# Expert weights in an MoE layer kernel: down pieces in a ring of their own, split late; a third result tile

## The chip, the cores and the metric

The kernel runs on one core of a Trainium2 chip, in one launch. The metric is the device time of that core in microseconds. A profiled execution is one more execution with the hardware profiler on; its rows are what this document argues from. Engines are named as in the profile: PE (matmul; PEld is its weight load), DVE (VectorE), ACT (ScalarE), POOL (GpSimd), SP (SyncE, which here only issues DMAs). "SPq" is SP's queue of instructions.

## The reference, cut to what matters

One layer: modulated RMSNorm, windowed attention beside a pooling mixer, output projection, residual; then a mixture of experts and a final RMSNorm. The change lies in the mixture of experts. All data are float32.

```python
D_MODEL, SEQ = 1024, 2048
N_EXPERTS, TOP_K, D_EXPERT = 64, 8, 256
def expert_block(args):                       # rows of tokens that chose expert e
    xb = h[tok_b]
    y = (jax.nn.silu(xb @ w_gate[e]) * (xb @ w_up[e])) @ w_down[e]
    return y.astype(F32) * w_b[:, None]
...
routed = zeros(T, D).at[row_tok].add(y_rows)  # gate-weighted, summed over a token's 8 experts
shared = (jax.nn.silu(h @ ws_gate) * (h @ ws_up)) @ ws_down
x = x + g2 * (routed + shared)
return rmsnorm(x, final_g)
```

## The kernel before

After attention and routing (to about 880 us of the span) the kernel runs one list of work, `run(work, ...)`: first the shared expert on 1024 tokens, then the 64 routed experts, large and small ones in turn (the table `CAPS` gives each rank of load a fixed number of rows, 640 down to 128), then the shared expert again on the other 1024 tokens with the final norm. An expert of up to 512 rows is one unit of work, a larger one two.

A unit n goes through these steps. `fetch` gathers its rows by an indirect DMA from POOL (xg<-X). `transpose_x` turns them on PE into xh and xl (PSUM tile tr). `ffn1` multiplies by gate and up weights (PSUM tile g, three of them) and makes fhh and fhl. `ffn2` multiplies by the down weights, in blocks of 128 rows and two halves of 512 columns (PSUM tile y, three of them); for each half DVE writes `yo = y * gate * g2` (line 1170), and after the second half POOL adds the 128x1024 tile into HBM by an indirect DMA (`scatter`, ACC<-yo, line 956). Each scatter waits for the landing of the one before, since all add into ACC. In program order unit n's `ffn2` stands behind `ffn1` of unit n+1.

Every float32 product is three matmuls of a high and a low part (`mm3`, lines 149 to 151). So every weight piece, a tile of 128x1024 (512 KB), is loaded by SP into a raw tile, then split: ACT copies it into the high part (line 145), DVE subtracts (line 146). An expert has six pieces: two of gate, two of up, two of down. Gate and up pieces become gu (six tiles, an expert needs four), down pieces wdh and wdl.

- Raw tiles (`raw_weights`, line 802): a ring of six, raw, and every seventh piece goes to a seventh tile, rawx, whatever it is.
- Results: two tiles yo.
- Down weights: three tiles each of wdh and wdl. `split_down` of expert si+1 stands in program order right behind `split_weights` of si+1.
- Loads: SP issues all six pieces of expert si+2 in the order gate, up, down, and then the row table of a later expert (tb). SP is a queue in order: a load whose raw tile is not free yet holds back all loads behind it.

A scheduler orders the instructions of each engine from this program and assigns the tiles of a ring, so the order on an engine is not that of the code; the order is fixed when the program is built.

Of the kernel before, what the change touches and what calls it, by code (L numbers as in the profile page):

```python
# [10 lines left out]
F32 = mybir.dt.float32  # L11
F32R = mybir.dt.float32r
# [8 lines left out]
P = 128  # L21
D = 1024
# [20 lines left out]
RAWS = 6  # L43
# [49 lines left out]
def layer(ctx: ExitStack, tc, a, rope, cpack, out, stop=99):  # L93
# [693 lines left out]
    with ExitStack() as ph:  # L787
# [11 lines left out]
        last = []  # L799
        pieces, more_raw = [], []  # L800
        g2 = small.tile([P, D], F32, name="g2", bufs=1)
# [3 lines left out]
        def raw_weights(g_src, u_src, d_src):  # L805

            def piece():

                pieces.append(1)
                if len(pieces) % (RAWS + 1) == 0:  # L810
                    if len(pieces) == RAWS + 1:
                        more_raw.append(rawp.enter_context(tc.tile_pool(name="m_rawx", bufs=1, reuse_waits="tile",
                                                                        side="right")))
                    return more_raw[0].tile([P, D], F32, name="rawx", bufs=1)
                return rp_.tile([P, D], F32, name="raw", bufs=RAWS)

            raws = []
            for src in (g_src, u_src):
                for half in range(2):
                    r = piece().rearrange("p (g f) -> p g f", g=2)  # L820
                    SY.dma_start(r, src[:, 2 * half:2 * half + 2])
                    raws.append(r)
            for f in range(2):
                r = piece()
                last[:] = [SY.dma_start(r, d_src[:, f, :])]
                raws.append(r)
            return raws

        def split_weights(raws, ins=None):
            gu = []  # L830
            for r in raws[:4]:
# [7 lines left out]
        def split_down(raws):  # L839
            wd = []  # L840
            for r in raws[4:6]:
                if len(raws) > 6:
                    V.tensor_tensor(r, r, g2, op=OP.mult)
                hi = wp2.tile([P, D], F32R, name="wdh", bufs=3)
                lo = wp2.tile([P, D], F32R, name="wdl", bufs=3)
                split(hi, lo, r)
                wd.append((hi, lo))
            return wd
# [110 lines left out]
        def shared_raw():  # L959
            return raw_weights(by_rows(a["ws_gate"][0:1]),  # L960
                               by_rows(a["ws_up"][0:1]),
                               a["ws_down"][0].rearrange("(c p) f -> p c f", p=P)) + ["scale"]

# [6 lines left out]
        def run(work, between, at):  # L970
# [6 lines left out]
            firsts = []  # L977
            raws = {0: work[0][0]()}
            xs = {0: fetch(*flat[0][3:5]), 1: fetch(*flat[1][3:5])}
            SY.dma_start(g2, bcast(MODS[0:1, 5 * D:6 * D]))  # L980
            gus = {0: split_weights(raws[0], firsts)}
            queue_after(tail["square"], firsts[1][0])
# [7 lines left out]
            for n, (si, ui, nu, rows, load, put) in enumerate(flat):  # L990
# [8 lines left out]
                if n == 0:  # L999
                    with tc.issue_after(lastx[0].ins):  # L1000
                        wds = {0: split_down(raws.pop(0))}
                    between(2)
                    raws[1] = work[1][0]()
# [12 lines left out]
                behind = functools.partial(ffn2, rows, *h, wds[si], put)  # L1016
# [130 lines left out]
        def slot(n, j):  # L1147
# [12 lines left out]
            for o, w in units(CAPS[j]):  # L1160
# [3 lines left out]
                def put(b, r, n, py, y, o=o, n_=n):  # L1164
                    q = (o + b) // P
                    gate = tabs[n_][:r, q, 1:2]
                    if n == 0:
                        y[0] = yp.tile([P, D], F32, name="yo", bufs=2)
                    sl = slice(n * 512, (n + 1) * 512)
                    V.scalar_tensor_tensor(y[0][:r, sl], py[:r], gate, g2[:r, sl], op0=OP.mult, op1=OP.mult)  # L1170
                    if n == 1:
                        scatter(y[0][:r], tabs[n_][:r, q, 0:1].bitcast(I32))
# [106 lines left out]
        def at(n, total, ask=False):  # L1279
# [3 lines left out]
            if u == 1:  # L1283
# [46 lines left out]
```

## Time and profile before

| | us |
|---|---|
| median of 3 runs (2668.33 to 2672.61) | 2668.43 |
| the profiled execution's own time | 2656.01 |
| its span, first to last instruction | 2654.2 |
| PE busy in the span | 2430.7 (92%) |
| DVE busy | 1841.1 (69%) |
| ACT busy | 1215.8 (46%) |
| POOL busy | 854.8 (32%) |
| mean share of the 16 DMA engines, 1015 to 2560 us | 0.83 |

The table's busy times come from the first part of the page, the last row from a view of stretches of time. "Idle before" and "waits" name what ended a wait, inferred from semaphores. In timelines the columns are start, duration, engine, line, operation, out<-in, count, and in brackets the idle time of the engine before the row with its releaser; equal instructions that follow each other are merged in one row, whose duration then runs over all of them. A matmul's recorded time is longer than its spacing, since matmuls are pipelined.

### The profile page before, as it was taken

Reading aid. Unit: us, or ns where it says so; the run is one execution under the profiler, and the core shown is the slowest. Engines: PE = TensorE matmul, PEld = TensorE weight load, DVE = VectorE, ACT = ScalarE, POOL = GpSimd, SP = SyncE. Lnnn points to the kernel's source line nnn. Section 1 sums busy time; section 2 is a strip of 40 time slices with the busy share of each in tenths; the row PEclk is TensorE's granted clock in tenths of the full one; section 3 lists DMA queues with packets and bytes.
Section 4 is the critical chain, followed back from the end, with each engine's and each line's share of the span. In section 5 each row is a group of like instructions: output and inputs, shape, how many; then the busy total and the mean of one; then the engine's idle time right before and its main releaser. Section 6 shows DMA issues by size and latency. Waiting matters only on the chain. (4 is left out here: it accounts for less than half of the span.)

```text
span 2654.2 us, 40459 instructions
## 1 busy us (share of the span) xinstructions
PE 2430.7 (92%) x14397; PEld 2102.8 (79%) x14397; DVE 1841.1 (69%) x3802; ACT 1215.8 (46%) x2052; POOL 854.8 (32%) x681
## 2 busy tenths in 40 slices
PE   6898978999999888999989989999999999999997
PEld 2776766777777677887778889989898888888886
DVE  7898766989899844556655656666665666667667
ACT  5322337777676433344333434444443444444443
POOL 3343332344443332232323332322333333333210
PEclk8999999999999999999989999999999999999998
DMA  7777559444454568778867878898887987888876
GB/s 253 217 243 235 180 159 279 140 140 132 139 152 126 182 190 200 198 225 229 240 181 216 229 200 247 220 273 232 238 247 214 272 242 233 233 248 242 231 204 248
DMA packets 266840, 564.53 MB, mean 213 GB/s; under 512 B 42966, under 2 KB 97950, under 8 KB 266636
## 3 DMA queue, kind: packets, MB, share of 16 engines
q1 hardware_dynamic: 177580, 350.08, 38.4%
q0 software_dynamic: 88768, 210.80, 34.7%
q8 instruction: 114, 1.87, 0.3%
q10 hardware_dynamic: 288, 1.05, 0.1%
q14 instruction: 90, 0.74, 0.1%
HBM read 408.83 MB, written 153.01 MB: 212 GB/s over the span
## 5 line engine op out<-in xcount | busy, mean ns | idle before, releaser
L149 PE MATMUL g<-xh,gu 128*128 128x256 f32 (+12 forms) x2112 | 670.8, 318 | 9.0 <-ACT xh L145 4.7
L150 PE MATMUL g<-xl,gu 128*128 128x256 f32 (+12 forms) x2112 | 658.4, 312 | 6.3 <-DVE xl L146 5.6
L151 PE MATMUL g<-xh,gu 128*128 128x256 f32 (+12 forms) x2112 | 658.0, 312 | 0.0
L956 POOL DMA_INDIRECT ACC<-yo,tb x165 | 307.3, 1862 | 932.1 <-DVE yo L1170 295.7
L149 PEld LDWEIGHTS g<-xh,gu 128*128 128x128 f32 x2112 | 405.9, 192 | 23.2 <-ACT xh L145 5.1
L150 PEld LDWEIGHTS g<-xl,gu 128*128 128x128 f32 x2112 | 406.7, 193 | 18.9 <-DVE xl L146 6.7
L1170 DVE SCALAR_TENSOR_TENSOR yo<-y,tb,g 128x512 f32<-128x512 f32 (+5 forms) x330 | 237.3, 745 | 255.6 <-DMA ACC<-yo,tb 203.5
L151 PEld LDWEIGHTS g<-xh,gu 128*128 128x128 f32 x2112 | 405.7, 192 | 8.7
L146 DVE TENSOR_TENSOR gu<-raw,gu 128x1024 fp32r<-128x1024 f32 x226 | 274.7, 1222 | 144.3 <-ACT gu L145 143.3
L149 PE MATMUL y<-wdh,fhh 128*128 128x512 f32 (+5 forms) x724 | 298.5, 413 | 63.8 <-DVE yo L1170 53.8
L145 ACT ACTIVATE gu<-raw 128x1024 fp32r<-128x1024 f32 x226 | 238.0, 1059 | 171.8 <-PE g L151 106.6
L150 PE MATMUL y<-wdl,fhh 128*128 128x512 f32 (+5 forms) x724 | 292.1, 404 | 0.0
L151 PE MATMUL y<-wdh,fhl 128*128 128x512 f32 (+5 forms) x724 | 291.3, 403 | 0.0
L146 DVE TENSOR_TENSOR xl<-tr,xh 128x512 fp32r<-128x512 f32 (+5 forms) x330 | 207.4, 648 | 80.7 <-ACT xh L145 80.1
L145 ACT ACTIVATE xh<-tr 128x512 fp32r<-128x512 f32 (+5 forms) x330 | 179.9, 566 | 161.4 <-PE tr L877 160.9
L952 POOL DMA_INDIRECT xg<-X,tb x165 | 180.8, 1096 | 160.0 <-PE tr L877 108.0
L145 ACT ACTIVATE wdh<-raw 128x1024 fp32r<-128x1024 f32 x114 | 116.6, 1053 | 231.8 <-PE y L151 230.8
L149 PEld LDWEIGHTS y<-wdh,fhh 128*128 128x128 f32 (+5 forms) x724 | 135.5, 187 | 107.1 <-DVE yo L1170 65.8
L877 PE MATMUL tr<-identr,xg 128*128 128x128 f32 (+6 forms) x1320 | 149.5, 243 | 27.3 <-DVE xl L146 24.4
L877 PEld LDWEIGHTS tr<-identr,xg 128*128 128x128 f32 (+6 forms) x1320 | 138.1, 141 | 43.6 <-DVE xl L146 29.4
L151 PEld LDWEIGHTS y<-wdh,fhl 128*128 128x128 f32 (+5 forms) x724 | 136.0, 188 | 36.2 <-issue 1.0
L150 PEld LDWEIGHTS y<-wdl,fhh 128*128 128x128 f32 (+5 forms) x724 | 136.2, 188 | 30.1 <-issue 0.5
(333 smaller groups left out, 4614.9 us busy)
## 6 DMA issues: line engine op xcount, KB each, us to landing
raw<-in_w_up_dram SPq DMA_DIRECT2D x110, 512.0 KB
raw<-in_w_down_dram SPq DMA_DIRECT2D x110, 512.0 KB
raw<-in_w_gate_dram SPq DMA_DIRECT2D x109, 512.0 KB
wa<-in_w_ada_dram SPq DMA_DIRECT2D x48, 512.0 KB
xt<-in_x_dram SPq DMA_DIRECT2D x32, 512.0 KB
kw<-Kd POOLq DMA_DIRECT2D x14, 768.0 KB, 8.0
rawx<-in_w_gate_dram SPq DMA_DIRECT2D x19, 512.0 KB
rawx<-in_w_up_dram SPq DMA_DIRECT2D x18, 512.0 KB
```

The source lines that it names most:

```text
L145: return (A.activation(hi, src, AF.Copy), E.tensor_tensor(lo, src, hi.bitcast(F32), op=OP.subtract))
L146: E.tensor_tensor(lo, src, hi.bitcast(F32), op=OP.subtract))
L149: T.matmul(ps, lh, rh, start=first, stop=False)
L150: T.matmul(ps, lh, rl, start=False, stop=False)
L151: T.matmul(ps, ll, rh, start=False, stop=last)
L877: T.transpose(tr[:, k, :r], xg[:r, (4 * u + k) * P:(4 * u + k + 1) * P], identr[:r, :r])
L952: G.indirect_dma_start(out=xg, out_offset=None, in_=X2, in_offset=bass.IndirectOffsetOnAxis(ap=idx, axis=0))
L956: G.indirect_dma_start(out=ACC, out_offset=bass.IndirectOffsetOnAxis(ap=idx, axis=0), in_=y, in_offset=None, compute_op=OP.add)
L1170: V.scalar_tensor_tensor(y[0][:r, sl], py[:r], gate, g2[:r, sl], op0=OP.mult, op1=OP.mult)
```

## The change

1. The down pieces leave the ring of raw: they get a ring of two, rawd. The ring raw keeps its six tiles, now for gate and up alone; rawx goes.
2. Down weights are split one expert later in program order: `down_of(si)` stands behind `ffn1` of expert si's own first unit (and behind `ffn2` of the unit before), no longer behind the gate and up split of si one expert earlier. wdh and wdl have two tiles each in place of three.
3. `load_weights(si + 2)` issues only gate and up pieces; the down pieces of si+1 are issued behind them by a closure that `raw_weights` returns.
4. Every third result tile is yox, a tile of its own, so results rotate over three tiles.
5. At the end, two of the tiles for the final norm come from the final pool ("room") in place of wdh and wdl.

The memory is the same: 7 + 6 + 2 = 15 tiles of 4 KB per partition before, 6 + 2 + 4 + 3 = 15 now.

```diff
-            def piece():
-                pieces.append(1)
-                if len(pieces) % (RAWS + 1) == 0:
...
-                    return more_raw[0].tile([P, D], F32, name="rawx", bufs=1)
-                return rp_.tile([P, D], F32, name="raw", bufs=RAWS)
             raws = []
             for src in (g_src, u_src):
                 for half in range(2):
-                    r = piece().rearrange("p (g f) -> p g f", g=2)
-                    SY.dma_start(r, src[:, 2 * half:2 * half + 2])
+                    r = rp_.tile([P, D], F32, name="raw", bufs=RAWS).rearrange("p (g f) -> p g f", g=2)
+                    last[:] = [SY.dma_start(r, src[:, 2 * half:2 * half + 2])]
                     raws.append(r)
-            for f in range(2):
-                r = piece()
-                last[:] = [SY.dma_start(r, d_src[:, f, :])]
-                raws.append(r)
-            return raws
+            def down():
+                ds = []
+                for f in range(2):
+                    r = rp_.tile([P, D], F32, name="rawd", bufs=2)
+                    last[:] = [SY.dma_start(r, d_src[:, f, :])]
+                    ds.append(r)
+                return ds
+            return raws, down
+        def out_tile(n):
+            if n is not None:
+                downs.append(n)
+                if len(downs) % 3 == 0:
...
+                    return more_room[0].tile([P, D], F32, name="yox", bufs=1)
+            return yp.tile([P, D], F32, name="yo", bufs=2)
...
-                hi = wp2.tile([P, D], F32R, name="wdh", bufs=3)
-                lo = wp2.tile([P, D], F32R, name="wdl", bufs=3)
+                hi = wp2.tile([P, D], F32R, name="wdh", bufs=2)
+                lo = wp2.tile([P, D], F32R, name="wdl", bufs=2)
...
-                if ui == 0 and si + 1 < len(work):
-                    gus[si + 1] = split_weights(raws[si + 1])
-                    wds[si + 1] = split_down(raws.pop(si + 1))
-                    if si + 2 < len(work):
-                        raws[si + 2] = work[si + 2][0]()
+                if ui == 0:
+                    if si:
+                        wds[si] = down_of(si)
+                    if si + 1 < len(work):
+                        gus[si + 1] = split_weights(raws.pop(si + 1))
+                        if si + 2 < len(work):
+                            load_weights(si + 2)
+                        if si:
+                            downs_in[si + 1] = downs_in[si + 1]()
...
-                        y[0] = yp.tile([P, D], F32, name="yo", bufs=2)
+                        y[0] = out_tile(n_)
...
-                        room += [wp2.tile([P, D], F32, name=t, bufs=3) for t in ("wdh", "wdl")]
+                        room += [fin["p"].tile([P, D], F32, name="room", bufs=2) for _ in range(2)]
```

What the scheduler makes of it on SP, at an expert of 352 rows in the middle of the list. The numbers tell tiles apart; the rows that load registers are left out. DVE in a wait means an earlier split, a DMAHW name the landing of a load some seven issues back. Before:

```order
L821 DMA raw_19322<-in_w_gate_dram 128x2x512 [waits DMAHW2_49,DMAHW0_49]
L821 DMA raw_19324<-in_w_gate_dram 128x2x512
L821 DMA raw_19326<-in_w_up_dram 128x2x512 [waits DMAHW3_49,DVE_49]
L821 DMA raw_19328<-in_w_up_dram 128x2x512 [waits DMAHW4_49,DVE_49]
L825 DMA raw_19330<-in_w_down_dram 128x1024 [waits DMAHW0_49,DVE_49]
L825 DMA raw_19332<-in_w_down_dram 128x1024 [waits DMAHW5_49,DMAHW1_49,DVE_49]
L1144 DMA tb_19334<-TAB_65 128x4 [waits DMAHW6_49,DMASW1_49,DMASW0_49]
L821 DMA rawx_19592<-in_w_gate_dram 128x2x512 [waits DMAHW7_49,DVE_49]
L821 DMA raw_19594<-in_w_gate_dram 128x2x512
L821 DMA raw_19596<-in_w_up_dram 128x2x512
L821 DMA raw_19598<-in_w_up_dram 128x2x512 [waits DMAHW2_49]
L825 DMA raw_19600<-in_w_down_dram 128x1024 [waits DMAHW3_49]
```

The same place now:

```order
L812 DMA raw_19310<-in_w_gate_dram 128x2x512
L812 DMA raw_19312<-in_w_gate_dram 128x2x512 [waits DMAHW7_49]
L812 DMA raw_19314<-in_w_up_dram 128x2x512 [waits DMAHW0_49]
L812 DMA raw_19316<-in_w_up_dram 128x2x512 [waits DMAHW1_49]
L1165 DMA tb_19318<-TAB_65 128x4 [waits DMAHW2_49,DMASW1_49,DMASW0_49]
L819 DMA rawd_19329<-in_w_down_dram 128x1024 [waits DMAHW4_49,DMAHW3_49,DVE_49]
L819 DMA rawd_19331<-in_w_down_dram 128x1024 [waits DMAHW5_49,DVE_49]
L812 DMA raw_19580<-in_w_gate_dram 128x2x512
L812 DMA raw_19582<-in_w_gate_dram 128x2x512 [waits DMAHW6_49]
L812 DMA raw_19584<-in_w_up_dram 128x2x512 [waits DMAHW7_49]
L812 DMA raw_19586<-in_w_up_dram 128x2x512 [waits DMAHW0_49]
L1165 DMA tb_19588<-TAB_65 128x6 [waits DMASW7_49,DMAHW1_49,DMASW6_49,DMASW5_49]
```

Before, the load into rawx_19592, a gate piece, waits for the split of the down piece rawx_19094 that held the tile, and the loads behind it, which wait for no split, queue behind that. Now the only loads that wait for DVE are the two down pieces, each for the split of the down piece before it in its tile; the four gate and up loads behind them wait for no split of their own. In SP's order the down pieces of one expert stand directly ahead of the gate and up pieces of the expert two further on.

ACT at the same expert (xh is an input part, sg and fhh belong to ffn1). Before:

```order
L145 ACTIVATE fhh_19349<-sg_19392 128x256 [waits DVE_49]
L145 ACTIVATE xh_19346<-tr_19467 128x4x96 [waits PE_49]
L145 ACTIVATE fhh_19350<-sg_19433 128x256 [waits DVE_49]
L145 ACTIVATE wdh_19309<-rawx_19094 128x1024 [waits DMAHW6_49,PE_49]
L145 ACTIVATE wdh_19575<-raw_19330 128x1024 [waits DMAHW4_49,PE_49,Activation_49]
L905 ACTIVATE sg_19653<-g_19621 128x352 [waits PE_49,Activation_49]
L145 ACTIVATE xh_19615<-tr_19646 128x4x128 [waits PE_49]
L145 ACTIVATE gu_19801<-rawx_19592 128x1024 [waits DMAHW7_49]
L145 ACTIVATE gu_19804<-raw_19594 128x1024 [waits DMAHW0_49]
```

Now:

```order
L145 ACTIVATE fhh_19337<-sg_19380 128x256 [waits DVE_49]
L145 ACTIVATE xh_19334<-tr_19455 128x4x96 [waits PE_49]
L145 ACTIVATE gu_19797<-raw_19580 128x1024 [waits DMAHW5_49,PE_49]
L145 ACTIVATE gu_19800<-raw_19582 128x1024 [waits DMAHW6_49,PE_49]
L145 ACTIVATE fhh_19338<-sg_19421 128x256 [waits DVE_49]
L145 ACTIVATE wdh_19551<-rawd_19329 128x1024 [waits DMAHW3_49,PE_49,Activation_49]
L145 ACTIVATE wdh_19555<-rawd_19331 128x1024 [waits DMAHW4_49,PE_49,Activation_49]
L912 ACTIVATE sg_19641<-g_19609 128x352 [waits PE_49,Activation_49]
L145 ACTIVATE xh_19603<-tr_19634 128x4x128 [waits PE_49]
```

The two wdh splits keep their place between two units of ffn1. Before, they were the second down piece of one expert and the first of the next; now they are the two of one expert. The gate split of the coming expert, which at this place stood behind the wdh splits and the first sg, stands ahead of them.

More of the change, by code (lines that the diff above doesn't have):

```diff
@@ L799, in layer @@
         last = []
-        pieces, more_raw = [], []
+        downs, more_room = [], []
         g2 = small.tile([P, D], F32, name="g2", bufs=1)
@@ L805, in raw_weights @@
         def raw_weights(g_src, u_src, d_src):
-            def piece():
-                pieces.append(1)
-                if len(pieces) % (RAWS + 1) == 0:
-                    if len(pieces) == RAWS + 1:
-                        more_raw.append(rawp.enter_context(tc.tile_pool(name="m_rawx", bufs=1, reuse_waits="tile",
-                                                                        side="right")))
-                    return more_raw[0].tile([P, D], F32, name="rawx", bufs=1)
-                return rp_.tile([P, D], F32, name="raw", bufs=RAWS)
             raws = []
@@ L819, in raw_weights @@
                 for half in range(2):
-                    r = piece().rearrange("p (g f) -> p g f", g=2)
-                    SY.dma_start(r, src[:, 2 * half:2 * half + 2])
+                    r = rp_.tile([P, D], F32, name="raw", bufs=RAWS).rearrange("p (g f) -> p g f", g=2)
+                    last[:] = [SY.dma_start(r, src[:, 2 * half:2 * half + 2])]
                     raws.append(r)
-            for f in range(2):
-                r = piece()
-                last[:] = [SY.dma_start(r, d_src[:, f, :])]
-                raws.append(r)
-            return raws
+            def down():
[10 more added lines that the diff above has]
+                if len(downs) % 3 == 0:
+                    if not more_room:
+                        more_room.append(rawp.enter_context(tc.tile_pool(name="m_yox", bufs=1, reuse_waits="tile",
+                                                                         side="right")))
+                    return more_room[0].tile([P, D], F32, name="yox", bufs=1)
+            return yp.tile([P, D], F32, name="yo", bufs=2)
         def split_weights(raws, ins=None):
             gu = []
-            for r in raws[:4]:
+            for r in raws:
                 w = wp.tile([P, 2, 4, DE], F32R, name="gu", bufs=6)
@@ L837, in split_weights, with split_down @@
             return [gu[:2], gu[2:]]
-        def split_down(raws):
+        def split_down(raws, scaled):
             wd = []
-            for r in raws[4:6]:
-                if len(raws) > 6:
+            for r in raws:
+                if scaled:
                     V.tensor_tensor(r, r, g2, op=OP.mult)
-                hi = wp2.tile([P, D], F32R, name="wdh", bufs=3)
-                lo = wp2.tile([P, D], F32R, name="wdl", bufs=3)
+                hi = wp2.tile([P, D], F32R, name="wdh", bufs=2)
+                lo = wp2.tile([P, D], F32R, name="wdl", bufs=2)
                 split(hi, lo, r)
@@ L961, in shared_raw @@
                                by_rows(a["ws_up"][0:1]),
-                               a["ws_down"][0].rearrange("(c p) f -> p c f", p=P)) + ["scale"]
+                               a["ws_down"][0].rearrange("(c p) f -> p c f", p=P))
         def shared_unit(o):
@@ L977, in run, with load_weights, down_of @@
             firsts = []
-            raws = {0: work[0][0]()}
+            raws, downs_in = {}, {}
+            def load_weights(s):
+                raws[s], downs_in[s] = work[s][0]()
+            def down_of(s):
+                return split_down(downs_in.pop(s), s in (0, len(work) - 1))
+            load_weights(0)
+            downs_in[0] = downs_in[0]()
             xs = {0: fetch(*flat[0][3:5]), 1: fetch(*flat[1][3:5])}
             SY.dma_start(g2, bcast(MODS[0:1, 5 * D:6 * D]))
-            gus = {0: split_weights(raws[0], firsts)}
+            gus = {0: split_weights(raws.pop(0), firsts)}
             queue_after(tail["square"], firsts[1][0])
@@ L1000, in run @@
                     with tc.issue_after(lastx[0].ins):
-                        wds = {0: split_down(raws.pop(0))}
+                        wds = {0: down_of(0)}
                     between(2)
-                    raws[1] = work[1][0]()
+                    load_weights(1)
+                    downs_in[1] = downs_in[1]()
                     xt[1], steps = transpose_x(xs.pop(1))
```

## The prediction

> **What bounds the kernel now.** First the page: how busy each engine is.
>
> ```profile
> span 2654.2 us, 40459 instructions
> PE 2430.7 (92%) x14397; PEld 2102.8 (79%) x14397; DVE 1841.1 (69%) x3802; ACT 1215.8 (46%) x2052; POOL 854.8 (32%) x681
> ```
>
> PE sets the pace, and only its idle time and its clock can be won. The change touches the routed experts alone, so next the view of stretches for these, in two stages (columns: stretch, length, busy time of PE, PEld, DVE, ACT, POOL, granted clock, DMA share, GB/s).
>
> ```profile
> 1015.00:1550.00 535.00, 498.39 (x2912) 439.33 (x2911) 314.12 (x415) 209.70 (x309) 163.91 (x110) 0.96 0.78 212
> 1550.00:2560.00 1010.00, 966.39 (x6357) 888.88 (x6356) 663.52 (x884) 446.31 (x662) 312.03 (x209) 0.98 0.85 242
> ```
>
> PE is idle for 535 - 498.39 = 36.6 us and 1010 - 966.39 = 43.6 us, 80 in all. The clock is short by 0.04 x 535 + 0.02 x 1010 = 41.6 us of full clock. These 122 us, less their overlap, are all that can be won. PE's waits in the first stage, then in the second, say who is late:
>
> ```profile
> PE y L149 <- DVE yo L1170: 17.4, 8, 3.9
> PE tr L877 <- DVE xl L146: 16.2, 6, 4.9
> ...
> PE y L149 <- DVE yo L1170: 35.5, 14, 5.5
> PE tr L877 <- DVE xl L146: 7.4, 5, 4.1
> ```
>
> PE waits for DVE, though DVE is busy only 978 of these 1545 us. So DVE, which works in order, is itself held. The waits of DVE, then of ACT, over both stages:
>
> ```profile
> DVE yo L1170 <- DMA ACC<-yo,tb: 197.9, 43, 8.1
> DVE gu L146 <- ACT gu L145: 188.4, 149, 6.9
> ...
> ACT gu L145 <- DMA rawx<-in_w_gate_dram: 48.1, 14, 9.3
> ACT gu L145 <- DMA raw<-in_w_gate_dram: 45.5, 27, 7.0
> ACT gu L145 <- DMA raw<-in_w_up_dram: 11.8, 6, 4.1
> ```
>
> There are two causes. One: DVE cannot write a result because the scatter of the result two blocks earlier hasn't landed. Two: ACT waits for a weight piece, DVE for ACT, and both stand in order before work that PE needs. An instance of the first (timelines of DVE and POOL):
>
> ```profile
> 1048.87 0.75 DVE L1170 SCALAR_TENSOR_TENSOR yo<-y,tb,g 128x512 f32<-128x512 f32 x1 [5.66 <-DMA ACC<-yo,tb]
> ...
> 1038.66 2.40 POOL L956 DMA_INDIRECT ACC<-yo,tb  x1 [6.66 <-DVE sg L922]
> 1049.48 1.58 POOL L956 DMA_INDIRECT ACC<-yo,tb  x1 [6.84 <-DMA ACC<-yo,tb]
> 1056.68 1.57 POOL L956 DMA_INDIRECT ACC<-yo,tb  x1 [4.32 <-DMA ACC<-yo,tb]
> ```
>
> The scatters run one at a time. And of the second (SP, ACT, DVE, PE):
>
> ```profile
> 1858.49 0.33 SPq L1144 DMA_DIRECT2D tb<-TAB  x1
> 1887.10 0.38 SPq L821 DMA_DIRECT2D rawx<-in_w_gate_dram  x1
> 1890.66 0.95 SPq L825 DMA_DIRECT2D raw<-in_w_down_dram  x2
> 1897.64 0.38 SPq L821 DMA_DIRECT2D raw<-in_w_gate_dram  x1
> ...
> 1893.92 1.06 ACT L145 ACTIVATE gu<-rawx 128x1024 fp32r<-128x1024 f32 x1 [6.39 <-DMA rawx<-in_w_gate_dram]
> 1905.07 1.06 ACT L145 ACTIVATE gu<-raw 128x1024 fp32r<-128x1024 f32 x1 [3.56 <-DMA raw<-in_w_gate_dram]
> ...
> 1885.86 1.21 DVE L146 TENSOR_TENSOR wdl<-rawx,wdh 128x1024 fp32r<-128x1024 f32 x1
> 1906.15 1.22 DVE L146 TENSOR_TENSOR gu<-raw,gu 128x1024 fp32r<-128x1024 f32 x1 [3.66 <-ACT gu L145]
> ...
> 1909.13 0.80 PE L149 MATMUL y<-wdh,fhh 128*128 128x512 f32 x1 [5.54 <-DVE yo L1170]
> 1910.15 0.63 PE L151 MATMUL y<-wdh,fhl 128*128 128x512 f32 x1
> ```
>
> SP issues nothing from 1858.8 to 1887.1: rawx still holds a down piece, whose split begins at 1885.86, and the loads behind wait in line. Then two experts' pieces come within 11 us, gate split follows gate load by 7 us, and PE stands for 5.54 us. After it the matmuls take 0.63 us. Because six pieces rotate over seven tiles, rawx falls to the first gate piece once in seven experts; SP's order confirms that place.
>
> **The change part by part.** *The third result tile.* A result now waits for the scatter three blocks back. The row at 1048.87 waited for the scatter issued at 1038.66; now it would need the one before, landed by then, since 1038.66 could not start earlier. In a burst of three or four blocks (an expert's ffn2) a tile gains one whole scatter, 7 to 10 us by the starts above (1038.66, 1049.48, 1056.68), and the longest wait of DVE is 8.1 us. So nearly all of this cause should go. Walking PE's gaps above 0.6 us in the timeline, I put about 31 us of the 80 on it, most in the first stage. Taken: -28.
>
> *Rings apart.* The 29 us hold on SP goes: no gate load waits for a down split of its own tile any more. The gaps behind late weights are about 44 us. Those at the rotation (PE stands 4 to 6 us, seven or eight times) should vanish. Taken: -40, before the cost below.
>
> *The clock.* It fell with the stalls (0.63 us matmuls right behind one). Of 41.6 us about half lies inside the idle time already counted. Taken: -16 of 20.
>
> *Down loads ahead of the gate loads.* This is the cost. The down loads now wait for both splits of the expert before, and behind them on SP stand four weight loads and a table; for the gate pieces ACT waits, for the tables POOL's gathers. An ordinary expert shows the time there is:
>
> ```profile
> 1955.40 2.01 ACT L145 ACTIVATE wdh<-raw 128x1024 fp32r<-128x1024 f32 x2 [3.23 <-PE y L151]
> 1956.76 2.35 DVE L146 TENSOR_TENSOR wdl<-raw,wdh 128x1024 fp32r<-128x1024 f32 x2
> 1958.00 1.52 SPq L821 DMA_DIRECT2D raw<-in_w_gate_dram  x2
> 1968.33 1.06 ACT L145 ACTIVATE gu<-raw 128x1024 fp32r<-128x1024 f32 x1 [0.65 <-PE g L151]
> 1969.77 1.06 ACT L145 ACTIVATE gu<-raw 128x1024 fp32r<-128x1024 f32 x1 [0.38 <-PE g L151]
> ...
> 1887.00:1889.00 2.00, 2.00 (x15) 2.00 (x14) 1.81 (x3) 0.53 (x2) 0.35 (x1) 1.00 0.58 63
> 1889.00:1892.00 3.00, 3.00 (x22) 2.98 (x21) 0.00 (x0) 0.00 (x0) 0.00 (x0) 1.00 1.00 233
> 1892.00:1899.00 7.00, 7.00 (x48) 6.96 (x47) 3.84 (x4) 4.77 (x7) 2.90 (x2) 1.00 1.06 398
> ```
>
> From the first wdl split done (1956.76 + 1.2 = 1958.0) to the two gate splits there are 10.3 and 11.8 us. What the burst of six loads at 1887.10 needed: nothing for 2 us, 3 us shared with an indirect DMA (233 GB/s in all), then 398 GB/s, which is 1.3 us for a piece of 0.52 MB. With half of the 233 for the weights, 0.35 MB are in by 1892, the third piece (1.57 MB) 3.1 us later, so 8 us after the first issue, the fourth at 9.3. ACT saw the first two 1 us later than this sum gives (1893.92 against 1892.5). So the gate pieces, now third and fourth, are usable about 9 and 10.3 us after the first down load: 1 us to spare on average. How late a split may be before PE feels it: at 1905.07 ACT waited 3.56 us and PE stood 5.54; the waits of about 1.5 us on other experts left PE 0 to 1.2 us idle. Bounds: zero if the pieces always make it; 2 us at each of some 45 experts with short units, 90 us, if they never do. I take 0.25 us x 45 = 11, near the lower end, because the mean arrival lies before the deadline, and a longer unit (half of the experts until 2300 us) leaves 4 us more.
>
> [...] The rate of 233 GB/s in the stretch with POOL's transfers agrees with sharing; the next stretch shows that the sharing ends after some 3 us.
>
> *Late split of the down pieces.* Same splits, same count, at the same place on ACT; two tiles are enough since both splits waited for the last ffn2 already ("ACT wdh" waits there, row at 1955.40), and a whole ffn1 covers them. Only at the last routed expert, where two ffn2 follow each other, PE waits for two splits: from 1955.40 to 1956.76 + 2.35 = 3.7 us, of which some part was there before. Taken: +2. The two "room" tiles cost nothing: their loads stand at the same place on SP.
>
> Sum: -28 - 40 - 16 + 11 + 2 = **-71 us** on the profiled execution, whose own time is 2656.0: 2585. The median of the runs is 12.4 above it, so **2597 us**.
>
> **The rivals.** *Late gates on most short experts* (gain partly given back): 1 us at 45 experts in place of 0.25, so 34 us less: 2631. For it: 1 us to spare is little. Against it: longer waits for weights than 1.5 us are seen only at the rotation.
>
> *Slower.* The two down pieces push the gate load past the tolerance on every short expert. It decides when the fourth piece takes over 13 us after the first down load, in place of 10.3: the gates' DVE subtract then stands in front of the evictions of y, PE stands about 2.5 us, and the clock falls with it, 1 us more. 3.5 x 45 = 158 less 84 won: +74, or 2742; with half of these experts hit, 79 - 84 + 2 + some clock, no change. For it: the sixth load of the burst did arrive late behind a scatter. Against it: the up loads that stood third and fourth at 1889 were split without a wait.
>
> *The scatter chain takes over.* Scatters run singly, and a third tile makes none faster.
>
> ```profile
> ACC<-yo,tb POOLq DMA_INDIRECT x165, 7.2
> ```
>
> At 7.2 us to landing and 0.7 to the next start, 162 need 1280 of 1545 us. If the denser weight bursts stretch one to 9.2 us, they need 1604, and nothing is won: about 2668. Against it: DVE waits for scatters for 198 us, not for most of the time, and the same bytes move.
>
> *The order does not change on chip*: excluded by SP's order.
>
> **How the numbers follow.** Forecast case 0.70 (2575 to 2620 alone), late gates 0.15, scatter chain 0.06, slower 0.09. The range of 8 in 10 goes from 2562 (all 80 us idle and 25 of clock won, nothing lost) to 2648. A measurement of this kernel tells 0.2%, 5 us, from no change. Faster 0.86: the first two cases and a little of the chain; same 0.05; slower 0.09.
>
> **What would show it.** In the profile after: DVE's waits for ACC from 198 us to below 50; no stretch of SP over 20 us without a load; ACT's waits for gate and up pieces together from 105 us to below 60, spread thinly over the experts; PE's waits in this stage below 25 us, clock 0.98 to 0.99. Wrong if ACT waits for gate pieces at nearly every expert, if ACC still holds DVE, or if PE's idle time falls without the span.

## The result and the profile after

The changed kernel takes 2584.38 us (median of 4 runs, 2572.22 to 2586.92) against 2668.38 for the kernel before (median of 4 runs as well; the table of the time before has three of them): a ratio of 0.969, 95% interval 0.9662 to 0.9718, or 84 us less. The forecast was 2597, with a range of 2562 to 2648. The profiled execution took 2586.92 us. Its page, and then the view of stretches (columns as before):

```profile
span 2585.0 us, 40372 instructions
PE 2411.0 (93%) x14397; PEld 2090.0 (81%) x14397; DVE 1850.9 (72%) x3802; ACT 1215.3 (47%) x2052; POOL 841.3 (33%) x681
```

```profile
1015.00:1500.00 485.00, 469.31 (x2755) 417.06 (x2756) 297.34 (x390) 200.73 (x297) 147.96 (x102) 0.97 0.79 221
1500.00:2480.00 980.00, 976.00 (x6542) 901.50 (x6541) 685.03 (x904) 455.85 (x678) 314.50 (x218) 1.00 0.90 254
2480.00:2585.00 105.00, 77.23 (x417) 65.62 (x415) 63.26 (x172) 31.82 (x56) 6.20 (x4) 0.90 0.65 205
```

PE is idle for 15.7 us in the first of these stages and for 4.0 in the second, where it was 36.6 and 43.6. The clock is short by 0.03 x 485 = 14.6 us in the first and by nothing in the second. The third row is the end, and there PE is idle for 28 us. The waits of PE in the three stages, then those of DVE and ACT that the prediction named (the routed experts), and SP's:

```profile
PE tr L884 <- DVE xl L146: 10.5, 4, 4.2
PE y L149 <- DVE yo L1191: 4.7, 1, 4.7
...
PE y L149 <- DVE yo L1191: 2.7, 3, 1.1
...
PE g L149 <- issue: 9.5, 1, 9.5
...
DVE yo L1191 <- DMA ACC<-yo,tb: 6.0, 3, 2.2
DVE yox L1191 <- DMA ACC<-yox,tb: 4.5, 1, 4.5
...
ACT gu L145 <- DMA raw<-in_w_gate_dram: 36.8, 23, 4.9
...
SPq L819 <- DVE wdl L146: 1071.1, 128, 39.3
```

DVE's waits for a scatter fell from 197.9 us to 10.5, ACT's for gate pieces from 93.6 to 36.8. SP now stands at the down loads (line 819) for 1071 us in all; the longest of these waits is 39.3 us, ahead of the first routed result, and 25.3 us among the routed experts. That SP stands is not new: before, the waits at its weight loads (lines 821 and 825) came to about 1150 us in the same stretch, up to 34.5 us. What is left is a group of four stalls between 1200 and 1370 us and one stall of 9.5 us behind the experts.

The two executions also differ ahead of the change. The first and the last write of a routed result, before and after (DVE):

```profile
1028.45 2.21 DVE L1170 SCALAR_TENSOR_TENSOR yo<-y,tb,g 128x512 f32<-128x512 f32 x3
...
2570.68 0.75 DVE L1170 SCALAR_TENSOR_TENSOR yo<-y,tb,g 128x512 f32<-128x512 f32 x1
```

```profile
1037.31 2.17 DVE L1191 SCALAR_TENSOR_TENSOR yo<-y,tb,g 128x512 f32<-128x512 f32 x3
...
2493.24 1.41 DVE L1191 SCALAR_TENSOR_TENSOR yox<-y,tb,g 128x512 f32<-128x512 f32 x2 [4.52 <-DMA ACC<-yox,tb]
```

The second row of after holds two writes; the last starts at 2493.91. So the part up to the first result took 8.9 us more (in the kernels below it ends anywhere from 1030 to 1039 on two of the chips, with the change or without, so I do not put this down to the change), the routed part 1456.6 us in place of 1542.2, 85.6 less, and the end, from there to the last instruction, 91.1 in place of 83.5, 7.6 more. In the routed part PE's idle time fell from 81.1 us to 19.2, and the time at half clock from 78.5 us to 27.3, which is 25.6 us of full clock. These lengths, taken in the same way from every profile, are used below: "routed" is the time from the first to the last write of a routed result, "end" the time behind it.

### The profile page after: what moved, and what is told of

Same layout as the page of the kernel before. It is cut to its first block, busy times and chain, and to the rows that moved or that the text cites. A ratio compares the mean times of both kernels' runs of the same rounds, so it can differ in the third digit from the quotient of the medians.

```text
span 2585.0 us, 40372 instructions
## 1 busy us (share of the span) xinstructions
PE 2411.0 (93%) x14397; PEld 2090.0 (81%) x14397; DVE 1850.9 (72%) x3802; ACT 1215.3 (47%) x2052; POOL 841.3 (33%) x681
## 5 line engine op out<-in xcount | busy, mean ns | idle before, releaser
L146 DVE TENSOR_TENSOR gu<-raw,gu 128x1024 fp32r<-128x1024 f32 x264 | 322.7, 1225 | 233.1 <-ACT gu L145 231.0
L149 PEld LDWEIGHTS g<-xh,gu 128*128 128x128 f32 x2112 | 400.8, 190 | 29.6 <-issue 10.1
L150 PEld LDWEIGHTS g<-xl,gu 128*128 128x128 f32 x2112 | 401.5, 190 | 15.9 <-DVE xl L146 4.2
L151 PEld LDWEIGHTS g<-xh,gu 128*128 128x128 f32 x2112 | 401.1, 190 | 8.6
L963 POOL DMA_INDIRECT ACC<-yo,tb x110 | 192.3, 1748 | 626.5 <-DVE yo L1191 155.8
L145 ACT ACTIVATE gu<-raw 128x1024 fp32r<-128x1024 f32 x264 | 279.1, 1059 | 213.9 <-PE g L151 156.4
L149 PE MATMUL y<-wdh,fhh 128*128 128x512 f32 (+5 forms) x724 | 292.2, 404 | 24.3 <-ACT yo L1049 11.3
L145 ACT ACTIVATE wdh<-rawd 128x1024 fp32r<-128x1024 f32 x132 | 132.9, 1053 | 270.3 <-issue 132.1
L1191 DVE SCALAR_TENSOR_TENSOR yo<-y,tb,g 128x512 f32<-128x512 f32 (+5 forms) x220 | 159.5, 745 | 50.5 <-PE y L151 43.4
L963 POOL DMA_INDIRECT ACC<-yox,tb x55 | 95.7, 1740 | 288.1 <-DVE yox L1191 49.6
L146 DVE TENSOR_TENSOR wdl<-rawd,wdh 128x1024 fp32r<-128x1024 f32 x132 | 155.3, 1215 | 21.7 <-ACT wdh L145 21.7
L884 PEld LDWEIGHTS tr<-identr,xg 128*128 128x128 f32 (+6 forms) x1320 | 138.4, 142 | 27.0 <-DVE xl L146 13.4
```

Source lines behind the costliest of these rows:

```text
L145: return (A.activation(hi, src, AF.Copy), E.tensor_tensor(lo, src, hi.bitcast(F32), op=OP.subtract))
L146: E.tensor_tensor(lo, src, hi.bitcast(F32), op=OP.subtract))
L149: T.matmul(ps, lh, rh, start=first, stop=False)
L150: T.matmul(ps, lh, rl, start=False, stop=False)
L151: T.matmul(ps, ll, rh, start=False, stop=last)
L884: T.transpose(tr[:, k, :r], xg[:r, (4 * u + k) * P:(4 * u + k + 1) * P], identr[:r, :r])
```

## The experiments

All times are in us. The kernels were measured in three groups, a, b and c, each on another chip; "before" is the kernel before on the chip of the group. On that of group b it took 2726, and the first routed result of the four kernels comes at 1089 to 1103 in place of 1028 to 1039, while the routed parts are no longer than elsewhere. So kernels of different groups are compared by ratio and by routed length. Lengths and idle times come from one profiled execution of each kernel. Two of the changed kernel differ by 1.6 us in the routed part, 4.2 in its idle time and 2.3 in the end; those of gate_first, on two chips, by 15.4 us in the routed part.

| kernel | group | median | before | ratio (95%) | routed | PE idle in it | end |
|---|---|---|---|---|---|---|---|
| before | | 2668.4 | | | 1542.2 | 81.1 | 83.5 |
| changed | | 2584.4 | 2668.4 | 0.969 (0.9662 to 0.9718) | 1456.6 | 19.2 | 91.1 |
| rings_only | a | 2636.6 | 2666.7 | 0.9874 (0.9832 to 0.9915) | 1508.1 | 56.7 | 87.2 |
| tile_wdl2 | a | 2641.4 | 2666.7 | 0.9896 (0.9854 to 0.9938) | 1512.4 | 60.4 | 94.7 |
| no_rot | a | 2663.6 | 2666.7 | 0.9985 (0.9959 to 1.0011) | 1543.9 | 81.3 | 82.7 |
| no_rot_tile | a | 2573.8 | 2666.7 | 0.9654 (0.9622 to 0.9687) | 1442.4 | 18.3 | 91.1 |
| no_rot_half | b | 2621.2 | 2726.2 | 0.9617 (0.9563 to 0.9671) | 1445.9 | 15.5 | 82.0 |
| gate_first | b | 2614.2 | 2726.2 | 0.961 (0.9554 to 0.9666) | 1425.1 | 0.9 | 91.9 |
| early512 | b | 2648.0 | 2726.2 | 0.9729 (0.9672 to 0.9787) | 1453.9 | 18.6 | 95.4 |
| no_rot_tile_early | b | 2640.1 | 2726.2 | 0.9696 (0.9643 to 0.9749) | 1433.2 | 11.8 | 102.0 |
| after_again | c | 2582.9 | 2669.2 | 0.9682 (0.9651 to 0.9712) | 1455.0 | 23.4 | 88.8 |
| gate_first_again | c | 2556.6 | 2669.2 | 0.9579 (0.9555 to 0.9603) | 1440.5 | 9.7 | 92.6 |
| no_rot_tile_again | c | 2583.2 | 2669.2 | 0.9689 (0.9654 to 0.9724) | 1440.8 | 15.9 | 93.1 |
| after_half | c | 2560.0 | 2669.2 | 0.9598 (0.9558 to 0.9637) | 1438.2 | 11.2 | 87.5 |

### One part of the change at a time

**rings_only**, the changed kernel with two result tiles:

```diff
-                if len(downs) % 3 == 0:
+                if len(downs) % 3 == 3:
```

> The changed kernel with two result tiles again; rings and late split stay. My theory (two separate causes, the third tile worth 28 us of idle time and about 8 of clock): 36 us slower than the changed kernel, about 2620, with DVE's waits for ACC back near 150 to 200 us. Rival, the rings do it all (DVE waited for the scatter only because late splits stood ahead of the results): 2585 to 2595, and DVE's waits for ACC below 60 us. Rival, the tile does it all: about 2660.

**tile_wdl2**, the kernel before with the third result tile. The memory for it comes from one wdl tile, so this is not the tile quite alone:

```diff
+        def out_tile(n): ...                  # as in the change
-                lo = wp2.tile([P, D], F32R, name="wdl", bufs=3)
+                lo = wp2.tile([P, D], F32R, name="wdl", bufs=2)
...
-                        y[0] = yp.tile([P, D], F32, name="yo", bufs=2)
+                        y[0] = out_tile(n_)
```

> The kernel before with the third result tile and nothing else but one wdl tile less, which pays for its memory; the rotation of six pieces over seven tiles stays. My theory: 28 us of idle time and 8 of clock won, about 2632; the gaps of 4 to 6 us at the rotation stay, the waits of DVE for ACC fall below 60 us. Rival, the tile does it all: 2590. Rival, the rings do it all: 2665.

The waits over 1015 to 2560 us, of rings_only and then of tile_wdl2 (of each those of PE, then DVE's for a scatter):

```profile
PE y L149 <- DVE yo L1191: 37.2, 17, 4.3
PE tr L884 <- DVE xl L146: 16.5, 5, 4.1
...
DVE yo L1191 <- DMA ACC<-yo,tb: 151.2, 39, 6.2
```

```profile
PE y L149 <- DVE yo L1181: 29.9, 14, 4.5
PE tr L888 <- DVE xl L146: 19.9, 9, 3.7
PE y L149 <- DVE yox L1181: 9.2, 6, 3.4
...
DVE yo L1181 <- DMA ACC<-yo,tb: 20.9, 5, 8.3
```

Alone, the rings win 34 us of the routed part and the tile 30. Both win less than was expected: 2637 us came in place of 2620 for the rings alone, 2641 in place of 2632 for the tile. The rivals, by which one of the two does it all, fell. But 34 and 30 make 64, and together the two win 86. The 22 us between are a result that the sum in the prediction has no place for. With the rings alone the stalls at the rotation are gone (between 1550 and 2290 us PE's longest gap is 2.4 us, 5.5 before), and in their place PE waits 17 times, 2.2 us each, for a result tile; with the tile alone DVE hardly waits for scatters any more (21.6 us in all), and the late weights stay. A part of the 22 us may be the wdl tile that tile_wdl2 lacks, which was not tried alone: ACT's waits for weight pieces are 154 us there, 105 before.

### Is it the rotation?

**no_rot**, the kernel before without the seventh raw tile; **no_rot_tile** has also the third result tile of tile_wdl2, with three wdl tiles:

```diff
-                if len(pieces) % (RAWS + 1) == 0:
+                if False:
```

> The kernel before without its seventh raw tile: six pieces over six tiles, so that each tile always takes the same piece; the early split and two result tiles stay. My theory (the rotation is the cause of the late weights, not the early split): as the changed kernel with two result tiles, about 2620, and no stretch of 20 us without a load on SP. Rival, the split's place is what counts, and one raw tile less makes weights later: 2668 or more.

> The kernel before without the seventh raw tile, whose memory goes to the third result tile: 6 raw, 6 wdh and wdl, 3 results, as many tiles as before. My theory: nearly all of the gain, 2585 to 2600, since both causes are gone. Rival, rings of their own and the late split are needed: 2630 or more, with PE's waits for xl and y behind late gate pieces as before.

no_rot, over 1015 to 2560 us, and behind it ACT's waits for gate pieces in no_rot_tile:

```profile
PE y L149 <- DVE yo L1170: 61.6, 29, 4.0
...
DVE yo L1170 <- DMA ACC<-yo,tb: 187.8, 41, 8.0
...
ACT gu L145 <- DMA raw<-in_w_gate_dram: 96.2, 47, 4.2
```

```profile
ACT gu L145 <- DMA raw<-in_w_gate_dram: 37.6, 26, 6.0
```

Taking the rotation away does what it should to SP: its longest wait among the routed experts falls from 34.5 us to 16.6. And yet nothing is won (0.9985, an interval that holds 1). PE's idle time is the same 81 us; 61.6 us of it are now 29 waits for DVE's write of a result, where before there were 22 waits of 52.9 us (the two rows in the prediction). With the third tile as well, the routed part is 100 us shorter than before. By the expectation, no_rot should have taken about 2620, the time then expected of rings_only. It took 2664, and the theory that had each cause stand by itself fell here. The rival, which came nearer with its 2668, blamed the early split and the missing raw tile; it fell with no_rot_tile, which has both and takes 2574.

**no_rot_half** asks whether the scatters had taken over. It is no_rot with scatters of half their rows, so that half of each routed result isn't added:

```diff
-                        scatter(y[0][:r], tabs[n_][:r, q, 0:1].bitcast(I32))
+                        scatter(y[0][:r // 2], tabs[n_][:r // 2, q, 0:1].bitcast(I32))
```

> The kernel before without its seventh raw tile, with two result tiles, and each routed scatter adds only the first half of its rows (the other rows of the result are left out). It asks why taking the rotation away won nothing. Theory, the scatter chain had taken over: a scatter takes fewer us, DVE's waits for ACC fall from 188 us to below 60, and the gain appears, 2575 to 2600. Rival, the early split and the tight raw ring still bring weights late: 2650 or more, with PE's waits as they were. Between: 2600 to 2650, both.

```profile
PE y L149 <- DVE yo L1170: 11.6, 13, 3.8
...
DVE yo L1170 <- DMA ACC<-yo,tb: 107.7, 39, 4.3
```

PE's waits for results fall from 61.6 us to 11.6, and the gain appears: the routed part is 98 us shorter than that of no_rot, with two result tiles, six raw tiles and the early split. DVE's own waits for scatters stay at 107.7 us, not below 60 as expected: shorter ones (4.3 us at most, 8.0 in no_rot) seldom reach PE. So in no_rot the scatters were what held the kernel. With half scatters the DMA engines were less busy, too (a share of 0.79 between 1500 and 2480 us, 0.86 in no_rot), so this run doesn't say that it was only the tile's wait; no_rot_tile, where scatters are whole and a tile more stands between, says it from the other side, with 18 us of idle time left.

So the two causes hide one another: these runs show that the gains do not add up. How it happens at each expert was not traced. My reading, argued and not shown, is that behind a late weight piece the scatters have caught up, and no tile is waited for; where weights come in time, the scatters are behind, and a third tile is needed to let DVE go on. In all, DVE waits for scatters about as long in both kernels (197.9 us before, 187.8 in no_rot). The rows show a link the other way round too. With the third tile, ACT's waits for gate pieces fall from 96.2 us to 37.6, though the raw tiles and the order of the loads are the same. That fits a DVE that stands for a scatter, splits late and so frees raw tiles late: a part of the late weights was the scatters' doing.

### What the order of the loads costs

The four stalls that are left look like this one in the changed kernel (SP, ACT, DVE, PE):

```profile
1166.73 1.47 SPq L819 DMA_DIRECT2D rawd<-in_w_down_dram  x2
1168.99 0.97 SPq L812 DMA_DIRECT2D raw<-in_w_gate_dram  x2
1170.14 1.00 SPq L812 DMA_DIRECT2D raw<-in_w_up_dram  x2
1172.45 0.35 SPq L1165 DMA_DIRECT2D tb<-TAB  x1
1192.60 1.47 SPq L819 DMA_DIRECT2D rawd<-in_w_down_dram  x2
1195.17 1.30 SPq L812 DMA_DIRECT2D raw<-in_w_gate_dram  x2
...
1203.94 1.06 ACT L145 ACTIVATE gu<-raw 128x1024 fp32r<-128x1024 f32 x1 [4.00 <-DMA raw<-in_w_gate_dram]
...
1205.02 1.22 DVE L146 TENSOR_TENSOR gu<-raw,gu 128x1024 fp32r<-128x1024 f32 x1 [4.37 <-ACT gu L145]
...
1206.91 0.54 PE L884 MATMUL tr<-identr,xg 128*128 128x128 f32 x4 [3.80 <-DVE xl L146]
```

ACT was free for the gate split 7.3 us after the first down load was issued (4.00 us before 1203.94) and got the piece at 11.3. The prediction had 10.3 us until the piece is needed and 9 until it is there. At the fourth stall PE waits for DVE's write of a result (the row of 4.7 us further up), behind a gate piece for which ACT waited 4.91 us.

**gate_first** puts the gate pieces of an expert ahead of the down pieces:

```diff
                         if si + 2 < len(work):
-                            load_weights(si + 2)
+                            ups_in.pop(si + 2)()
+                        if si + 3 < len(work):
+                            load_gates(si + 3)
                         if si:
                             downs_in[si + 1] = downs_in[si + 1]()
```

> The changed kernel with the gate pieces of an expert issued ahead of the down pieces that stood in front of them (order on SP: gate, down, up, table). Theory, the four stalls of about 4 us between 1200 and 1365 us come from the down loads ahead in the queue: the gates land two pieces, 2.6 us, earlier, which takes about 10 us with the clock, 2575. Rival, gates are late because they share with scatters and gathers: 2584 unchanged. Rival, up pieces, now behind, come late in their place: 2590 or more.

> The changed kernel once more, on the chip and in the call of the next three, so that they can be compared with it. Both theories of the next runs expect its ratio to the kernel before as it was, 0.966 to 0.972, with late gate pieces stopping PE about four times between 1200 and 1370 us and some 9 us at the barrier behind the experts.

after_again came out so: 0.9682, with four stalls of 3.3 to 4.9 us at the same places, and 5.9 us at the barrier in place of 9.

> The kernel with gate pieces ahead of down pieces, beside the changed kernel. Its profile in the first run had none of the four stalls. Theory, the order on the queue is what the change lost: 15 us of idle time and 10 of clock less than the changed kernel, ratio 0.959 to 0.962. Rival, the stalls were absent by chance of that chip: the same as the changed kernel within 5 us, and the stalls are there again.

SP and ACT of gate_first_again at the same expert, its waits (ACT to 2500 us, DVE to 2560), and the stretch in which the stalls were, of this kernel and then of the changed one:

```profile
1176.64 4.07 SPq L812 DMA_DIRECT2D raw<-in_w_gate_dram  x2
1193.76 1.48 SPq L825 DMA_DIRECT2D rawd<-in_w_down_dram  x2
...
1195.39 1.06 ACT L145 ACTIVATE gu<-raw 128x1024 fp32r<-128x1024 f32 x1 [0.43 <-PE g L151]
```

```profile
ACT gu L145 <- DMA raw<-in_w_gate_dram: 2.8, 2, 1.4
...
DVE yo L1208 <- DMA ACC<-yo,tb: 113.5, 35, 7.6
DVE yox L1208 <- DMA ACC<-yox,tb: 45.6, 15, 5.8
```

```profile
1200.00:1500.00 300.00, 300.00 (x1771) 266.66 (x1770) 199.35 (x263) 130.42 (x193) 104.36 (x69) 1.00 0.85 243
```

```profile
1200.00:1500.00 300.00, 284.80 (x1588) 249.04 (x1587) 180.34 (x235) 119.48 (x175) 91.72 (x63) 0.95 0.79 224
```

This kernel beats the changed one: on the same chip 2556.6 against 2582.9, 26 us less, as gate_first_again expected (25); in group b its ratio is 0.961, but the changed kernel has no run there. The expectation of gate_first had only 10 us, because it counted the two pieces ahead in the queue, 2.6 us. The rows show another size: the tile of the first gate piece is free at 1176.64, while in the changed kernel the loads stand until 1195.17 behind two down loads, which wait for the splits of the down pieces before. SP held the first for 18.5 us, not for 2.6. (The trace of the changed kernel says the same by itself: the split that frees this tile ends there at 1175.45.) PE has no idle time at all from 1200 to 1500, and the full clock. The profiled execution of this kernel was the slowest of its five (2573.36); in it two stalls of 2.4 and 2.3 us stand at 2155 and 2247, behind a DVE that waits for a scatter again.

DVE waits for scatters for 159 us there, with three tiles, though PE is idle for only 9.7 us of the routed part. In the profiled execution of gate_first, the fastest of its four, these waits are 35.4 us, and PE is idle for 0.9 us in the whole routed part. It is busy for 1425.1 - 0.9 = 1424.2 us of it, and the changed kernel's 1456.6 - 19.2 = 1437.4, less half of its 27.3 us at half clock, make 1423.7; so by this estimate gate_first lost about nothing to the clock there, and little but PE's own work is left to shorten.

**no_rot_tile_again** stands beside these:

> Six raw tiles without rotation and the third result tile, early split, beside the changed kernel. Theory, it is faster than the changed kernel by about 9 us: 5 at the barrier (its down splits of the last expert stand earlier), 4 in fewer late gates. Rival: the two are equal within 3 us and the difference seen was one of chips.

On one chip it equals the changed kernel (0.9689 and 0.9682), though on different chips it had seemed 10 us faster: the rival held. So a ring of its own for the down pieces, with the late split, is worth no more than the plain ring of six, when three result tiles are there.

### The end

Behind the last expert a loop for overflowing experts stands, with no turn here, at which all engines meet. POOL and PE of the changed kernel there, and then of the kernel before:

```profile
2485.05 1.55 POOL L963 DMA_INDIRECT ACC<-yox,tb  x1 [6.88 <-DVE wdl L146]
2493.87 1.55 POOL L963 DMA_INDIRECT ACC<-yo,tb  x1 [7.27 <-issue]
2500.71 1.55 POOL L963 DMA_INDIRECT ACC<-yo,tb  x1 [5.29 <-DVE fhl L146]
2507.60 1.55 POOL L963 DMA_INDIRECT ACC<-yox,tb  x1 [5.34 <-DMA ACC<-yo,tb]
...
2515.48 0.79 PE L149 MATMUL g<-xh,gu 128*128 128x512 f32 x1 [9.48 <-issue]
```

```profile
2576.28 1.56 POOL L956 DMA_INDIRECT ACC<-yo,tb  x1 [5.23 <-DMA ACC<-yo,tb]
...
2584.04 0.50 PE L149 MATMUL g<-xh,gu 128*128 128x512 f32 x1 [2.50 <-issue]
```

The write of the last result ended at 2494.65, its scatter could start 13 us later, and PE went on at 2515.48. The brackets of three of the changed kernel's four scatters name other releasers. But where the trace has the landing of a scatter, at 2484.32 and at 2506.87, the next starts 0.73 us behind it, at 2485.05 and at 2507.60: a scatter waits for the one before. From 2285.40 to 2507.60 us there are 27 of them, 8.5 us from start to start.

The same two places in every profile say where the end got longer. From the last write's start to the row at which PE goes on it takes 13.4 us before and 21.6 in the changed kernel; from there to the last instruction 70.1 and 69.5. With two result tiles and whole scatters the first stretch is 13.4 to 15.6 us (before, no_rot, rings_only), and one scatter starts in it; with three it is 19.7 to 22.1 in seven profiles, with the early split or the late one, and two scatters start in it (the two kernels with an early unit of 512 rows, below, left aside). So what the end lost is one more scatter in line, which the third tile allows.

**after_half**, the changed kernel with scatters of half their rows (the edit of no_rot_half; half of each routed result isn't added):

> The changed kernel in which each routed scatter adds only the first half of its rows (the other rows of the result are left out). Theory, the scatters standing in line at the end set the barrier: the 9.5 us at the barrier go, with 5 of clock, and nothing between 1500 and 2480 us changes, since PE is busy there: 12 to 20 us below the changed kernel if the late gates stay, 25 to 40 if they go too because the loads no longer share with scatters. Rival, the barrier waits for something else: less than 5 us won and the stall at the barrier stays.

```profile
PE g L149 <- ACT gu L1282: 2.2, 1, 2.2
PE tr L884 <- DVE xl L146: 4.3, 3, 1.7
```

The 9.5 us (5.9 in after_again) became 2.2, with another releaser: the barrier waits for the scatters. From the last write to PE's going on it takes 17.1 us. The kernel is 23 us faster than after_again, between the two ranges that were expected, but little of this is the end's: by the profiles 16.8 us are won in the routed part, 6.1 ahead of it and 1.3 in the end. In the routed part the late gates shrank (waits of 1.7 us at most for xl, 4.2 in the changed kernel) but didn't go. Gate pieces landed there 7.2 us after their issue (median of 128), in the changed kernel 8.7.

**early512** gives PE 256 rows more to do ahead of that barrier, and **no_rot_tile_early** does the same in the other kernel. The line shown is not all of the edit: the stored results take the two gu tiles into which the final norm loaded ahead, so that it has four such tiles in place of six.

```diff
-        fins = [(256, 1024, early_put), (512, 1280, final_put(1280)), (256, 1792, final_put(1792))]
+        fins = [(512, 1024, early_put), (256, 1536, final_put(1536)), (256, 1792, final_put(1792))]
```

> The changed kernel with the last shared expert's early unit, whose results are stored until the scatters are done, of 512 rows in place of 256, and two units of 256 behind it. Theory, PE's 9.5 us at 2506 us are the scatters that still stand in line when the experts are through: 17 us more matmuls ahead of the barrier hide them, 9.5 us and 5 us of clock less, about 2570. Rival, the final norm of 16 tiles behind the barrier sets the end, whatever PE does: 2580 to 2590.

> The kernel before without the seventh raw tile, with the third result tile and with the early unit of 512 rows. Theory: its 5 us at the barrier and 2 us of clock go, about 2566. Rival, the final norm sets the end: 2574 or more.

The stall at the barrier went, to 2.2 us in both. The end became longer: 95.4 against 91.1 and 88.8 of the changed kernel, 102.0 against 91.1 and 93.1 of no_rot_tile. Neither is faster by ratio (0.9729, 0.9696) than the kernel that it came from. Behind the row at which PE goes on, 66.4 and 67.3 us are left, though PE is busy there for only 35.2 and 36.7 us, in place of 52.3 in both kernels that they came from. So PE's work is not what sets this stretch, as the rival had it. That the loads, norms and stores of the 16 last tiles set it is the rival's reading, and was not followed further; nor was what the two tiles less cost.

## Why the prediction was right, and where it was not

**Sum.** -71 was forecast on the profiled execution, and -69 is what the two profiled executions differ by. That match is luck: 9 us were lost ahead of the routed part, and the medians differ by 84. Errors of the terms cancel, too. In the routed part PE's idle time fell by 62 us, where its terms (-28, -40, +11) make 57; the clock gave 25.6 us in place of 16; the end cost 7.6 in place of 2. The direction, the order of size and the two causes were right; the gain was under-sized by 13 us.

**Two causes, 31 and 44 us.** Both were there: each edit wins alone (30 and 34 us of the routed part, of which 20.7 and 24.4 are idle time). What failed is that the sum treated them as separate. I put each gap of PE down to the one cause that ended it. That gives the right total for taking both away (idle time 81 to 19), and too much credit to either alone: no_rot, which takes only the rotation away in its plainest form, wins nothing, because the scatters end the waits in its place.

**The third tile, -28.** The waits that it was to take went: DVE's for scatters are 21.6 us in tile_wdl2 and 10.5 now. But its worth is no fixed number: 20.7 us of idle time alone, 37.5 beside the rings (rings_only to the changed kernel), 63.0 in no_rot. The reason given, that a tile gains one scatter, fits the runs, and fits the end, where one scatter more stands in line.

**Rings apart, -40.** The stalls at the rotation vanished; but rings of their own were not needed for that, since no_rot_tile does as well. That no stretch of SP over 20 us without a load would be left was wrong: there are three, up to 25.3 us. The clock of 0.98 to 0.99 that I named came out as 0.97 in the first stage and 1.00 in the second.

**Down loads ahead of the gate loads, +11.** The step that failed most. The cost was right in kind and wrong in place and size. I took 0.25 us at 45 experts, from the time between splits at one expert at 1955 us. (A small slip in the same sum: ACT saw the first piece 1.4 us later than reckoned, by its own numbers, not 1.) In that part the gate pieces do come in time: ACT waits 16 times, 17.1 us in all, between 1500 and 2480, and PE is idle for 4.0. The price is paid at four places of the first stage, where an expert of 128 rows (256 at the fourth) follows one of 448 to 512, and ACT, in the instance shown, is ready after 7.3 us, not 10.3, and gets the piece at 11.3, not 9. It is 3.8 + 4.2 + 2.1 + 4.7 = 14.8 us of idle time and 27.3 us of half clock behind them, 28 us in all; gate_first_again wins 26 back. And SP holds the gate loads until the down tiles are free, for 18.5 us in the instance shown.

**The upper bound, 90 us.** No run shows the 2 us at each of 45 experts behind it; 28 us were paid. That the weights get half of the rate beside an indirect DMA was my estimate. In the trace of the kernel before they had less: from 1889 to 1892 us the queue of SP's loads (q1) moved 0.29 MB of 0.70 and that of the indirect DMAs (q0) 0.41, and from 1892 to 1897 q1 moved 1.98 MB of 2.00, at 400 GB/s in all. With half scatters (after_half) gate pieces land sooner, after 7.2 us in place of 8.7, so the scatters do bear on them. But in the instance shown the larger part of the wait was the 18.5 us on SP; from issue to split it took 8.8 us.

**The clock, -16.** Mis-sized: 25.6 us. I had put half of the loss inside idle time. In the trace before, all but 13 of the 78.5 us at half clock lie behind the stalls, in pieces of 3.4, 6.8 and once 10.2 us; and the four stalls of the changed kernel, 14.8 us in all, went with 27.3 us at half clock, 13.7 us of full clock, so that these few large stalls cost nearly as much again as their own length.

**The late split, +2.** The end costs 7.6 us more (5.3 in after_again). For the late split alone 2 was about right: rings_only, with two result tiles, takes 15.6 us from the last write to PE's going on, 13.4 before. The rest is a term that the sum does not have: the third tile lets one more scatter stand in line at the barrier. With half scatters this stretch is 17.1 us, still 3.7 more than before; why stays open.

**The rivals.** "Late gates on most short experts" happened at few of them. "The scatter chain takes over" was given 0.06, and it is what happened where only the rotation was taken away, and what stands at the end of the changed kernel; it didn't take the gain because the third tile covers it. "Slower" didn't come near: ACT waits 2.3 to 4.9 us for the first gate piece, but at four places only.

## What to carry to other kernels

When two things hold an engine, each gap in the trace names the one that came last; what taking one away wins is known only when the other's next arrival is worked out too. Here two edits of 30 and 34 us won 86 together, and a third, which looked like the cause, won nothing alone.

In the changed kernel a down load that waited for its tile held the gate loads behind it on SP until 1195.17, though the tile of the first was free by 1176.64, 18.5 us before: look for the load with the longest wait and put those that are needed sooner ahead of it. That was 26 us here, by moving two loads.

A buffer more in front of a serial chain lets the work run ahead, but the chain still has to end: look at what waits for its last link.

## What the runs showed of the hardware

In the routed part of the kernel before, the granted clock fell to half with stalls of PE of 1.96 and 2.25 us, for 3.4 us each time, and with all nine of 3.8 to 5.5 us, for 6.8 us with seven of them; three of 2.3 to 2.6 us were followed by no half clock. So the length of a stall did not by itself tell what came behind it. Every piece of half clock in the traces of this kernel and of the changed one lasts 3.41, 6.83 or 10.24 us, or stands at the very end. The stall of 2.08 us that ended at 1309 in the changed kernel was followed by 6.8 us at half clock: 3.4 us of full clock lost, 5.5 in all.

Half as many rows did not halve a scatter. The median from issue to landing was 6.9 us for the scatters from yo and 8.9 us for those from yox in the changed kernel, and 5.4 and 6.7 us in after_half.
